# Turning the outputs of the first attention pair in the PSUM bank of another role

## The chip, the cores and the metric

One core of a Trainium2 chip runs the whole kernel as a single program. The metric is device time in microseconds (us), the median of several executions. One more execution is profiled. All durations below come from that one.

## The reference

The kernel computes one inference step of a small backbone: two layers (DEPTH = 2), model width 1024, on 128 context tokens and 512 latent tokens. A layer has four mixers side by side, whose outputs are concatenated and go through one projection `w_out`; then comes a gated feed-forward part.

```
h = rmsnorm(x, g_pre1) * (1 + scale1) + shift1
aq, ak, av, bq, bk, bv, cz, cx, cb, cc, cdt, du = split(h @ w_in)
ya = rmsnorm(diff_attention(aq, ak, av, lam), a_subln) * (1 - lam_init)   # 4 heads, two softmaxes each
yb = gqa_attention(bq, bk, bv)                                            # 4 query heads, 2 key heads
yc = ssd_mixer(cz, cx, cb, cc, cdt, ...)                                  # chunked scan, forward and backward
yd = s5_mixer(du, ...)
x = x + gate1 * rmsnorm(concat(ya, yb, yc, yd) @ w_out, g_post1)
h = rmsnorm(x, g_pre2) * (1 + scale2) + shift2
g, v = split(dwconv(h @ w_up))
x = x + gate2 * rmsnorm((silu(g) * v) @ w_down, g_post2)
```

## The kernel before

**The stages of a layer.** Projections from `w_in`, then the four mixers, then `w_out`, the norm, and the feed-forward part with `w_up` and `w_down`. The mixers are written one behind the other in `mixer` (S5, its GLU, `ssd` for the SSD scan, then `attention`), but they run interleaved: each piece of code carries a priority (`PR`: S5 0, GLU 10000, attention 20000, scan 30000, projections 40000; the smaller goes first), and a scheduler writes out one fixed list of instructions for each engine when the program is built. At run time each engine takes its list strictly in order.

**PSUM.** The eight banks are shared out by role (`pss`, L149): two of role p, two of role e, one of v, one of u, two of d. A request for a bank of a role gets the next buffer of that role in the order in which the requests stand in the code, and waits until the request that had this buffer last has been read out. So a request for d that `attention` makes stands behind every request for d that `ssd` made, whenever either runs. A matrix product of `ssd` goes to a bank of d throughout: the transposes of its inputs, eight state updates (L985 to L996), then for each of the five chunks of 128 tokens the scores, the decays and the outputs (L1003 to L1056), and last the sums and the spread of its norm.

**The attention.** It has six units (`units`, L1349): the first pair (0,0,0) and (0,0,1), two heads of the differential attention, below A0; then (1,0), two heads of the grouped attention, G0; then the second pair A1 and (1,1), G1. A unit is a list of fronts (scores, maxima, exponentials) and backs (transposes of the probabilities, products with the values). A back takes the probabilities in groups of four blocks of 128 by 128: four transposes into one bank (L1209, "weights turned"), a copy of the high part by ScalarE and of the low part by VectorE into SBUF (L155, L156), then eight products into the bank of role v. The bank of the weights comes from `self.tb`:

```
self.tb, self.work = itertools.cycle("u"), itertools.cycle([pool])
...
                if i == 3:
                    self.tb = itertools.cycle("ud")
```

So up to G0 all weights are turned in the single bank u; from A1 on (and in the last group of G0) u and d alternate. When the second head of a pair or of a G unit is done, its last back turns the outputs (`self.oo`, a tile `at_o` of which there is one buffer): four transposes into one bank, a fifth into the next (L1321), read by L1324 and L1325 into the rows of `h` that `w_out` multiplies. The next unit's first back (`prompt_back`) asks for `at_o` again, turns the weights of the prompt (`at_pp`, L1209), multiplies them in the same bank, and writes the result from the bank to `at_o` (`put`, L1223 and L1224). It can write only when the transposes of the outputs before have read `at_o`.

**What runs beside.** The first product with `w_out` (rows 6 and 4 of `h`: k = 6, 7 from S5, k = 4, 5 from the scan) and, in layer 0 alone, the modulation products (tile `wm`) fill TensorE in bank p.

Of the kernel before, what the change touches and what calls it, by code (L numbers as in the profile page):

```python
# [72 lines left out]
class K:  # L73
# [1069 lines left out]
    def attn_unit(self, l, pool, kq, kind, u, m0=0):  # L1143
# [61 lines left out]
        def turned(srcs, ps):  # L1205

            n = 128 * len(srcs)
            for j, s in enumerate(srcs):
                nc.tensor.transpose(ps[:, 128 * j:128 * j + 128], s, self.c("ident"))  # L1209
            w = next(self.work)  # L1210
            eh, el = (w.tile([P, 512], F32R, tag=t, name=t, bufs=2)[:, 0:n] for t in ("at_h", "at_l"))
            self.split(eh, el, ps[:, 0:n])
            return [(eh[:, 128 * j:128 * j + 128], el[:, 128 * j:128 * j + 128]) for j in range(len(srcs))]

        def values(o, e, kt, first, last):
            self.mm(o, e[0], vhl[:, kt, :], first, False)
            self.mm(o[:, 0:64], e[1], vhl[:, kt, 0:64], False, last)

        def put(O, ps):

            n = ps.shape[-1] // 128
            o = ps.rearrange("p (t x d) -> p t x d", t=n, x=2)
            A.copy(O, o[:, :, 0, :])  # L1223
            V.tensor_add(O, O, o[:, :, 1, :])  # L1224
# [4 lines left out]
        def small():  # L1229
            return pool.tile([P, 16], F32, tag="at_s", name="at_s", bufs=4)  # L1230
# [62 lines left out]
        def back(m, qt):  # L1293
            if qt == 0:
                st["out"], st["todo"] = self.pss("v"), []
            p, todo, out = st[m, qt], st["todo"], st["out"]
            todo += [(qt, kt, p[:, 128 * kt:128 * kt + 128]) for kt in range(5)]
            while len(todo) >= 4:
                group = todo[:4]
                del todo[:4]  # L1300
                for (t, kt, _), e in zip(group, turned([g[2] for g in group], self.pss(next(self.tb)))):
                    values(out[:, 128 * t:128 * t + 128], e, kt if kt < 4 else 5, kt == 0, kt == 4)
            if qt < 3:
                return
            o = O[m]
            put(o[:, 0:4, :], out)
            V.tensor_mul(o, o, rz[m].unsqueeze(2).to_broadcast([P, 5, 64]))
            if kind == 0:
                sq = pool.tile([P, 512], F32, tag="at_c", name="at_q")[:, 0:320].rearrange("p (t d) -> p t d", t=5)
                G.tensor_mul(sq, o, o)  # L1310
                ss = small()[:, 0:5]
                V.reduce_sum(ss, sq, axis=AX.X)
                r = self.rsqrt(pool, ss, 5, 64, "a")
                G.tensor_mul(o, o, r.unsqueeze(2).to_broadcast([P, 5, 64]))
            if m == 0:
                return
            for ts in ((0, 1, 2, 3), (4,)):
                ps = self.pss(next(self.tb))
                n = 128 * len(ts)
                for k, t in enumerate(ts):  # L1320
                    nc.tensor.transpose(ps[:, 128 * k:128 * k + 128], self.oo[:, t, :], self.c("ident"))  # L1321
                hi, lo = (t[:, CH[ts[0]]:CH[ts[0]] + n] for t in self.h[2 * u + kind])
                if kind == 0:
                    A.activation(hi, ps[:, 0:n], AF.Identity, scale=self.subg)  # L1324
                    V.scalar_tensor_tensor(lo, ps[:, 0:n], self.subg, hi.bitcast(F32), op0=ALU.mult, op1=ALU.subtract)  # L1325
                else:
                    self.split(hi, lo, ps[:, 0:n])
        return [(prompt_front, prompt_back)] + [(partial(front, m, qt), partial(back, m, qt)) for m in heads for qt in range(4)]

    @staticmethod  # L1330
# [480 lines left out]
```

## Time and profile before

| | us |
|---|---|
| median of 3 runs | 2189.75 |
| lowest and highest | 2186.13, 2194.58 |
| the profiled execution's own time | 2191.5 |
| its span, first to last instruction | 2189.7 |
| TensorE busy | 1956.1 (89%) |
| VectorE busy | 1245.6 (57%) |
| ScalarE busy | 802.4 (37%) |
| GpSimd busy | 676.4 (31%) |
| mean granted TensorE clock (1 is 2.4 GHz) | 0.898 |

The profile lists instructions by engine with start and duration, what ended an engine's idle time, and the chain of work that ended last, followed back from the end. A busy share is a mean over stages that have different limits. Here two stretches of the span are read, one in each layer, in which attention and scan run: 320 to 552 us and 1420 to 1650 us. In the lists PE is TensorE, DVE VectorE, ACT ScalarE and POOL GpSimd.

### The profile page before, as it was taken

The page shows a single profiled execution, that of the slowest core. Times are in us where ns is not written, and L with a number is a line of the kernel's source. Part 1 is how long each engine was busy: PE and PEld are TensorE (multiplying, and loading weights), DVE is VectorE, ACT ScalarE, POOL GpSimd, SP SyncE. Part 2 cuts the span into 40 slices and gives each one's busy share as a digit, 9 for nine tenths or more (in the row PEclk, how much of TensorE's full clock was granted, in tenths as well). Part 3 has the DMA queues.
Part 4 walks back from the last instruction along what each step waited for, and adds up shares of the span by engine and source line. Part 5 has one row for each costly group of instructions (what it writes and reads, how often), then busy time and mean ns, then how long its engine had stood idle before and what let it go on. Part 6 is the DMA issues. An engine that isn't in the chain of part 4 may idle for free.

```text
span 2189.7 us, 33260 instructions
## 1 busy us (share of the span) xinstructions
PE 1956.1 (89%) x12812; PEld 1786.6 (82%) x12812; DVE 1245.6 (57%) x2879; ACT 802.4 (37%) x1614; POOL 676.4 (31%) x723
## 2 busy tenths in 40 slices
PE   5996789999699999999988797897985999999997
PEld 2895775876597888999988786876875999999996
DVE  6876785475768575233366475653847631323345
ACT  3423353443452223232343244442444533313241
POOL 3553424200433352122244232323104332212232
PEclk9997789888799999999988887886866999999998
DMA  7464325134305665222224521310112012222221
GB/s 295 136 207 160 114 74 177 40 101 131 107 20 185 197 223 190 85 77 73 91 79 149 184 98 61 117 45 10 51 40 95 20 56 80 73 82 70 75 87 49
DMA packets 93511, 230.29 MB, mean 105 GB/s; under 512 B 17960, under 2 KB 30888, under 8 KB 93352
## 3 DMA queue, kind: packets, MB, share of 16 engines
q1 hardware_dynamic: 82856, 213.46, 29.8%
q10 hardware_dynamic: 10496, 14.71, 1.9%
q8 instruction: 101, 1.65, 0.3%
q14 instruction: 58, 0.48, 0.1%
HBM read 192.21 MB, written 35.92 MB: 104 GB/s over the span
## 4 chain that ended last, share of the span: by engine, by line
PE 67%; DVE 15%; DMA 9%; ACT 3%; issue 2%; POOL 2%; SPq 1%; ACTq 0%; POOLq 0%; DVEq 0%
PE psb L81 34%; PE psp L81 12%; PE psd L81 7%; PE pse L81 6%; PE psv L81 5%; DMA s_tb<-s5td 2%; DMA wm<-in_w_mod 1%; DVE nt L391 1%; PE psu L1209 1%; DMA wr<-in_w_down 1%; DVE x L394 1%; DMA ck<-in_cache_ak 1%; DVE wl L98 1%; DMA q<-d_bq 1%; DVE at_s L1279 1%
## 5 line engine op out<-in xcount | busy, mean ns | idle before, releaser
L81 PE MATMUL psb<-hh,wh 128*128 128x256 f32 (+1 forms) x1152 | 359.1, 312 | 2.3 <-DVE cv L451 2.3
L81 PE MATMUL psb<-hl,wh 128*128 128x256 f32 (+1 forms) x1152 | 358.3, 311 | 0.0
L81 PE MATMUL psb<-hh,wl 128*128 128x256 f32 (+1 forms) x1152 | 357.3, 310 | 0.0
L98 POOL TENSOR_TENSOR wl<-wr,wh 128x1024 fp32r<-128x1024 f32 (+3 forms) x87 | 192.3, 2211 | 502.7 <-ACT wh L95 451.6
L95 ACT CAST wh<-wr 128x1024 fp32r<-128x1024 f32 (+3 forms) x174 | 168.6, 970 | 417.9 <-PE psb L81 283.4
L81 PEld LDWEIGHTS psb<-hh,wh 128*128 128x128 f32 x1152 | 217.9, 189 | 13.3 <-issue 8.2
L81 PE MATMUL psp<-hh,wh 128*128 128x386 f32 (+1 forms) x640 | 215.3, 337 | 10.7 <-ACT hh L374 7.8
L81 PEld LDWEIGHTS psb<-hl,wh 128*128 128x128 f32 x1152 | 218.7, 190 | 3.4 <-issue 3.4
L81 PEld LDWEIGHTS psb<-hh,wl 128*128 128x128 f32 x1152 | 218.1, 189 | 3.4 <-issue 3.4
L81 PE MATMUL psp<-hl,wh 128*128 128x386 f32 (+1 forms) x640 | 209.8, 328 | 0.1
L81 PE MATMUL psp<-hh,wl 128*128 128x386 f32 (+1 forms) x640 | 207.0, 324 | 0.3 <-POOL wl L98 0.3
L98 DVE TENSOR_TENSOR wl<-wr,wh 128x1024 fp32r<-128x1024 f32 (+3 forms) x87 | 100.1, 1151 | 144.0 <-ACT wh L95 143.6
L81 PE MATMUL psb<-uh,wh 128*128 128x256 f32 (+1 forms) x544 | 169.9, 312 | 0.0
L81 PE MATMUL psb<-ul,wh 128*128 128x256 f32 (+1 forms) x544 | 169.4, 311 | 0.0
L81 PE MATMUL psb<-uh,wl 128*128 128x256 f32 (+1 forms) x544 | 169.1, 311 | 0.0
L81 PE MATMUL pse<-k,q 96*128 96x128 f32 (+5 forms) x288 | 107.1, 436 | 44.6 <-ACT at_p L1195 15.1
L81 PEld LDWEIGHTS psp<-hh,wh 128*128 128x128 f32 x640 | 129.0, 202 | 17.4 <-ACT hh L374 8.8
L81 PEld LDWEIGHTS psp<-hl,wh 128*128 128x128 f32 x640 | 129.3, 202 | 2.6 <-issue 1.1
L81 PEld LDWEIGHTS psp<-hh,wl 128*128 128x128 f32 x640 | 128.6, 201 | 1.4 <-issue 0.5
L1419 POOL TENSOR_TENSOR cv<-cv,cv 128x642 f32<-128x642 f32 x44 | 71.6, 1629 | 170.5 <-DVE cv L451 141.2
L81 PEld LDWEIGHTS pse<-k,q 96*128 96x128 f32 (+2 forms) x288 | 60.5, 229 | 77.7 <-issue 32.5
L450 DVE SCALAR_TENSOR_TENSOR cv<-psb,vec,cv 128x641 f32<-128x641 f32 x72 | 63.5, 881 | 103.2 <-ACT cv L449 103.2
(525 smaller groups left out, 4741.7 us busy)
## 6 DMA issues: line engine op xcount, KB each, us to landing
wm<-in_w_mod SPq DMA_DIRECT2D x96, 512.0 KB
wr<-in_w_up SPq DMA_DIRECT2D x88, 512.0 KB
wr<-in_w_in SPq DMA_DIRECT2D x30, 512.0 KB
wr<-in_w_down SPq DMA_DIRECT2D x32, 384.0 KB
wr<-in_w_down SPq DMA_DIRECT2D x32, 320.0 KB
wr<-in_w_out SPq DMA_DIRECT2D x16, 512.0 KB
s_tb<-s5td SPq DMA_DIRECT2D x8, 992.0 KB
s_to<-s5td SPq DMA_DIRECT2D x8, 768.0 KB
```

What stands on the lines that cost most here:

```text
L81: self.nc.tensor.matmul(out, w, x, start=start, stop=stop)
L95: nc.scalar.copy(hv, rv)
L98: e.tensor_sub(lv, rv, hv.bitcast(F32))
L391: nc.vector.scalar_tensor_tensor(t, y[c][:, t0:t1], gg[:, c, g:g + 1], r(t0, t1), op0=ALU.mult, op1=ALU.mult)
L394: (nc.gpsimd if c % 2 else nc.vector).tensor_add(xs, xs, t)
L450: nc.vector.scalar_tensor_tensor(out[:, 1:TW], x[:, 0:TW - 1], w[:, 0:1], out[:, 1:TW], op0=ALU.mult, op1=ALU.add)
L1209: nc.tensor.transpose(ps[:, 128 * j:128 * j + 128], s, self.c("ident"))
L1279: V.reduce_max(s[:, k:k + 1], ps, axis=AX.X)
L1419: G.tensor_mul(cv[0], cv[0], cv[1])
```

## The change

In the last back of a pair or G unit, the bank for the outputs of A0 (kind 0, u 0) is now asked of role d, and no longer of `self.tb`, which gives u there. Nothing else is written differently.

```
-                ps = self.pss(next(self.tb))
+                ps = self.pss("d" if kind == 0 and u == 0 else next(self.tb))
```

It concerns two banks and five transposes in each layer. The scheduler's lists move more than these. Three places on TensorE follow (psu, psd, psp are tiles in banks u, d and p; identr is the identity; at_o the outputs of A0; at_pp the weights of the prompt of G0; sd_, cf and nsq tiles belong to the scan, rq_y to its norm; wm to the modulation).

TensorE, layer 0, before: the outputs of A0 and the first weights of G0.

```order
L1321 MATMUL psu<-identr,at_o 128x128 x4
L81 MATMUL psd<-cst,sd_md 128x128 x4
L81 MATMUL pse<-k,q 128x128 x8
L81 MATMUL psp<-wm,sc 32x512 x2
L81 MATMUL psd<-sd_ex,sd_xd 64x128
L81 MATMUL psd<-cst,sd_small 64x128 x8
L1321 MATMUL psu<-identr,at_o 128x128
L81 MATMUL psp<-wm,sc 32x512 x2
L81 MATMUL psd<-sd_ex,sd_xd 64x128 x7
L81 MATMUL psd<-cf_2523,sd_h_3171 128x128
L81 MATMUL psd<-cf_2523,sd_h 128x128
L81 MATMUL psp<-wm,sc 32x512 x2
```

The outputs stand within the first chunk of the scan, and the first weights of G0 right behind.

TensorE, layer 0, with the change: the same outputs (hh_88 is row 4 of `h`, from the scan).

```order
L81 MATMUL psd<-cst,sd_md 128x128 x8
L81 MATMUL psd<-sd_ex,sd_xd 64x128 x8
L81 MATMUL psd<-cst,nsq 128x1 x10
L81 MATMUL psd<-identr,rq_y 128x128 x5
L1321 MATMUL psd<-identr,at_o 128x128 x4
L81 MATMUL psp<-hh_88,wh 128x256
L81 MATMUL psp<-hh_88,wh 128x386
L1321 MATMUL psd<-identr,at_o 128x128
L81 MATMUL psp<-hl_89,wh 128x256
L81 MATMUL psp<-hh_88,wl 128x256
L81 MATMUL psp<-hl_89,wh 128x386
L81 MATMUL psp<-hh_88,wl 128x386
```

The outputs now stand behind the last row of the scan's norm; in the list they moved from place 1219 to place 1369. The first weights of the prompt of G0 stand early, at 1204; its second ones, which stood at 1238, are at 1383, and all 40 blocks of probabilities of G0 follow them, with 96 rows of `w_out` (k = 4, 5) in between.

TensorE, layer 1, with the change: the end of the scan and the outputs of A0, which stood at place 6258 and 6405 before, the first weights of G0 at 6406.

```order
L81 MATMUL psd<-cf_13089,cf_12934 128x128 x2
L81 MATMUL psd<-cst,sd_md 128x128 x8
L81 MATMUL psd<-sd_ex,sd_xd 64x128 x8
L81 MATMUL psd<-cst,nsq 128x1 x10
L81 MATMUL psd<-identr,rq_y 128x128 x5
L1321 MATMUL psd<-identr,at_o 128x128 x4
```

The same turn of the order: outputs at 6549, the second weights of the prompt at 6563, then G0.

## Rows read from the trace of the kernel before

**Rows 1.** The page: the chain that ended last, shares by engine.

```profile
PE 67%; DVE 15%; DMA 9%; ACT 3%; issue 2%; POOL 2%; SPq 1%; ACTq 0%; POOLq 0%; DVEq 0%
```

**Rows 2.** Busy us by stretch: PE, PEld, DVE, ACT, POOL; granted clock, DMA share, GB/s.

```profile
409.40:433.80 24.40, 20.15 (x138) 17.58 (x138) 6.78 (x19) 9.29 (x22) 6.65 (x8) 0.86 0.07 22
433.80:446.00 12.20, 11.56 (x47) 10.94 (x47) 11.24 (x32) 5.73 (x17) 1.01 (x1) 0.50 0.01 2
446.00:513.60 67.60, 61.63 (x321) 38.91 (x319) 39.96 (x118) 28.33 (x92) 6.73 (x7) 0.88 0.43 134
513.60:551.60 38.00, 37.97 (x253) 35.05 (x253) 25.15 (x60) 16.34 (x39) 2.39 (x1) 0.89 0.35 110
1542.10:1609.70 67.60, 59.09 (x354) 52.68 (x352) 51.90 (x137) 31.70 (x95) 11.44 (x9) 0.88 0.15 49
```

**Rows 3.** Busy us by stretch of the weights turned alone (L1209): PE, PEld.

```profile
409.40:433.80 24.40, 0.64 (x4) 0.61 (x5) 0.86 0.07 22
...
1474.60:1530.70 56.10, 0.00 (x0) 0.20 (x1) 0.71 0.04 10
```

**Rows 4.** Timeline of PE, layer 0, attention: start, us, instruction, count.

```profile
344.03 0.66 PE L1321 MATMUL psu<-identr,at_o 128*128 128x128 f32 x4
...
349.58 0.33 PE L1321 MATMUL psu<-identr,at_o 128*128 128x128 f32 x1
...
409.38 0.66 PE L1209 MATMUL psu<-identr,at_p 128*128 128x128 f32 x4
...
433.80 1.06 PE L1209 MATMUL psd<-identr,at_p 128*128 128x128 f32 x4
...
446.04 1.06 PE L1321 MATMUL psu<-identr,at_o 128*128 128x128 f32 x4
...
513.64 1.11 PE L1321 MATMUL psu<-identr,at_o 128*128 128x128 f32 x4
...
551.60 0.63 PE L1321 MATMUL psu<-identr,at_o 128*128 128x128 f32 x4
```

**Rows 5.** Timeline of POOL and PE, layer 0, scan and first row of `w_out`.

```profile
328.99 1.18 POOL L971 TENSOR_TENSOR sd_xd<-sd_xt,sd_small 128x256 f32<-128x256 f32 x2 [0.99 <-DVE sd_small L946]
...
340.31 0.69 PE L81 MATMUL psd<-cf,cf 64*128 64x128 f32 x4
...
356.17 0.49 PE L81 MATMUL psd<-cf,cf 64*128 64x128 f32 x2
...
438.41 0.88 PE L81 MATMUL psp<-hh,wh 128*128 128x256 f32 x2
```

**Rows 6.** Timeline of PE, layer 1, attention.

```profile
1413.26 0.27 PE L1321 MATMUL psu<-identr,at_o 128*128 128x128 f32 x1
...
1427.38 1.12 PE L1209 MATMUL psu<-identr,at_p 128*128 128x128 f32 x4 [0.45 <-DVE at_o L1224]
...
1542.13 0.97 PE L1321 MATMUL psu<-identr,at_o 128*128 128x128 f32 x4
...
1648.48 1.09 PE L1321 MATMUL psu<-identr,at_o 128*128 128x128 f32 x4 [1.53 <-DVE at_o L1307]
```

**Rows 7.** Timeline of POOL and PE, layer 1, scan, and the first weights behind it.

```profile
1436.92 1.19 POOL L971 TENSOR_TENSOR sd_xd<-sd_xt,sd_small 128x256 f32<-128x256 f32 x2 [2.53 <-DVE sd_small L946]
...
1456.73 0.49 PE L81 MATMUL psd<-cf,cf 64*128 64x128 f32 x4
...
1476.73 0.48 PE L81 MATMUL psd<-cf,cf 64*128 64x128 f32 x2 [0.51 <-DVE sd_ea L1050]
...
1489.17 0.48 PE L81 MATMUL psd<-cf,cf 64*128 64x128 f32 x2 [0.51 <-DVE sd_ea L1050]
...
1530.71 1.06 PE L1209 MATMUL psd<-identr,at_p 128*128 128x128 f32 x4
```

**Rows 8.** Timeline of PE, layer 0: two rows of `w_out` that follow each other.

```profile
447.95 0.34 PE L81 MATMUL psp<-hh,wl 128*128 128x386 f32 x1
448.13 0.34 PE L81 MATMUL psp<-hh,wh 128*128 128x386 f32 x1
```

## The prediction

> **What bounds the kernel now.** I read the page first: TensorE carries 67% of the chain that ended last [rows 1]. That is a mean over the span, so I went on to the two stretches that the change touches, with the busy shares by stretch, and then to the timeline there. In layer 0 attention and scan run interleaved from about 340 us, where the scan's first chunk begins (340.31) [rows 5]. G0 (the grouped unit behind the first pair) turns its last single-bank group of weights at 409.38; the next group stands in bank d at 433.80 [rows 4]. In between VectorE works 6.78 of 24.40 us and ScalarE 9.29 [rows 2]; only four transposes of weights are in that stretch, those of 409.38, and in layer 1 there are none at all from 1474.6 to 1530.7 [rows 3]. The attention stands still there, because its next group asks for a bank of role d, and every request of the scan for d is ahead of it. As soon as the scan has ended, the attention goes on. So the end of this stage is set by the scan's end first, then by what is left of the attention: G0's outputs at 446.04, those of A1 at 513.64, those of G1 at 551.60 [rows 4]. In layer 1 the same chain reads 1530.71 [rows 7], 1542.13 and 1648.48 [rows 6]. From G0's outputs to those of G1 it is 105.6 us in layer 0 and 106.4 in layer 1. After that the last products with `w_out` and the norm wait for G1's outputs, so a shift of these passes on to the end.
>
> **What the change does.** It adds no instruction and takes none away: the same five transposes, copy and VectorE operation in each layer, in another bank. What it moves is a wait. The outputs of A0 need a bank of role d, and the requests of the scan for d come first in the code. So these transposes, which stood in the middle of the scan's first chunk, wait for the scan's last rows, as the list of TensorE shows. Behind them waits the single buffer `at_o`: the first back of G0 has multiplied its prompt weights early, but cannot write the result, and holds bank u meanwhile. All 40 blocks of probabilities of G0 are turned in that bank, or in d, so nearly all of G0 now runs after the scan, where before nine groups of ten ran beside it. The old wait of the attention before A1 goes away, because the scan is over by then; the new one, before G0, is longer. No DMA is added; on SP's queue the loads of `w_out` weights move with their rows, and I cost that at nothing, because the rows of k = 4, 5 wait for the scan's result in any case; if a load came late, it would show as idle time of TensorE behind the scan.
>
> **The scan's end.** Without G0 beside it the scan is faster. How fast it runs alone is seen in layer 1, after the attention stopped: one chunk takes 1489.17 - 1476.73 = 12.4 us, and the four last chunks with the norm take 1530.71 - 1476.73 = 54.0 us [rows 7].
> - Layer 0: the first chunk takes 356.17 - 340.31 = 15.9 us [rows 5], with the tail of A0 and the modulation beside it. That stays. The other four and the norm at the pace of layer 1: 356.2 + 54.0 = 410.2, against 433.80.
> - Layer 1: its state updates take from 1436.92 to 1456.73, 19.8 us, with G0 beside them [rows 7]; the same work takes 340.31 - 328.99 = 11.3 us in layer 0, with less of the attention beside it [rows 5]. So 1436.9 + 11.3 + 12.4 + 54.0 = 1514.6, against 1530.71.
> - Bounds: no gain at all (433.8 and 1530.7), since rows of `w_out` and of the modulation still stand between those of the scan; downwards some 3 us in each, if the first chunk in layer 0 takes 12.4 too.
>
> **G0 alone.** No row shows G0 with the scan over. The nearest is G1, a unit of the same kind with nothing but `w_out` beside it: from A1's outputs to its own 551.60 - 513.64 = 38.0 us [rows 4], TensorE busy all of it at a clock of 0.89 [rows 2]. Three things differ. Behind the scan the clock is low: the stretch of 12.2 us that follows it now is granted 0.50, that is 1.2 GHz, after a stretch in which the engine was partly idle [rows 2]; what takes 12.2 us there takes 6.9 at 0.89, so 5.3 more. TensorE's list then has rows of `w_out` that need the scan's own result; the first of them starts 438.41 - 433.80 = 4.6 us after the scan's end [rows 4, 5], and the second prompt weights stand behind it: 4.6 more. And the groups have one bank in place of two; I take 3 us. Sum 51. The other end is the length G0 has now: 409.38 - 349.58 = 59.8 us from A0's last output to the ninth group, and 446.04 - 433.80 = 12.2 for the rest [rows 4], 72 in all, with the scan beside it. The lower end is 38. I take 51, because G1 is the nearest row: the scan is over.
>
> **What follows.** From G0's outputs on everything stands as before: 105.6 and 106.4 us. The two stretches up to A1's outputs took 67.6 us both, although TensorE, VectorE and DMA had different work in them [rows 2], so I take them as a chain that does not mind what fills TensorE. The 96 rows of `w_out` that now run beside G0 leave this stretch; at 0.18 us a row at most (447.95 to 448.13 [rows 8]) that is 17 us of TensorE, which is the bound for a gain there. I take 0.
>
> **The sum.** Layer 0: 410.2 + 51 - 446.0 = 15.2 later. Layer 1: 1514.6 + 51 - 1542.1 = 23.5 later. Together 38.7 us. Against the profiled execution's own time of 2191.5 that gives 2230; the median of the runs shown is 1.75 below that execution, so 2189.75 + 38.7 = 2228. I predict **2228 us**. A difference of 0.5%, 11 us, is about what a measurement of this kernel can tell from no change.
>
> **Rivals.**
> - *G0 alone is as quick as G1.* Then it takes 38.0: layer 0 410.2 + 38.0 - 446.0 = 2.2, layer 1 1514.6 + 38.0 - 1542.1 = 10.5; 2202 us. For it: prompt scores and the first front of G0 are computed while it waits. Against it: the low clock behind the scan.
> - *G0 stays as slow as now.* 72 us: 42 more than the forecast, 2270 us. For it: in layer 0 modulation rows, whose weights come by DMA, fall between its groups. Against it: VectorE and ScalarE lose the scan's work.
> - *The new bank frees the attention: faster.* If the outputs got a buffer of d between two of the scan's requests, bank u would be free for G0's weights at once. In layer 0 the 5.6 us between the two output turns (344.03 and 349.58 [rows 4]) would go; in layer 1 G0 would no longer wait from 1413.26, the fifth output, to 1427.38, its first group [rows 6], and the scan would be alone sooner and end up to 16 us earlier (1514.6). 5.6 + 16 gives 2168 us. The Trainium skill (Perfetto Trace Analysis, section Matmuls) speaks for this: independent groups of matmuls should rotate through different banks, so that reading out one overlaps the next, and this change does that for outputs and weights; by that rule the sum would be 2168, by the rows it is 2228. The point that decides is whether the request waits behind the scan's. Here it does: the attention's next request for d waited until 433.80, though only four transposes ran in the 24.4 us before [rows 3, 4], and the lists put the outputs behind the norm. A bank that is another one is not a free one.
> - *Less filling in A1's stretch.* The 96 rows pay back all of their 17 us in each layer: 2228 - 34 = 2194, no change. Against it the two equal 67.6.
>
> **How the numbers follow.** Forecast, with G0 between 44 and 60 us: 0.60. G0 as quick as G1: 0.14. The filling pays back: 0.06. G0 as slow as now: 0.14. Freed attention: 0.06. The range leaves out the freed attention, the upper two thirds of the slow case and the lower part of the payback, under 0.2 in all: 2198 to 2258. Faster by over 0.5% is the freed attention alone, 0.06. Within 0.5% are the payback and over half of the quick case, whose 12.7 us lie at the limit: 0.14. Slower: 0.80.
>
> **What would show it.** In the timeline of TensorE after the change: the transposes at L1321 in bank d begin right after the scan's norm, near 410 in layer 0, and in layer 1 near 1515 plus the shift of layer 0; no group of weights (four transposes, `at_p`) of G0 stands between A0's outputs being ready and that moment; G0's outputs come some 51 us later; and A1's stretch is still near 67.6. That shift is 15 us. The prediction is wrong if transposes at L1321 in bank d start while products of the scan still follow, if the scan ends where it ended, or if G0 takes under 45 us.

## The result and the profile after

The changed kernel is slower by more than twice what was forecast: a median of 2298.72 us (2295.05 to 2302.01, 4 runs) against 2192.16 us (2186.13 to 2196.34, 4 runs) for the kernel before on the same chip, a ratio of 1.0488 with a 95% interval of 1.0455 to 1.0521. That is 107 us more; the forecast was 38, its range ended at 2258. The profiled executions differ by 2294.6 - 2189.7 = 104.9 us of span.

The page after has nearly the same work; TensorE's busy time grew by 40.5 us, at a lower mean clock (0.876, before 0.898).

```profile
span 2294.6 us, 33282 instructions
...
PE 1996.6 (87%) x12812; PEld 1814.8 (79%) x12812; DVE 1242.6 (54%) x2879; ACT 804.5 (35%) x1614; POOL 676.4 (29%) x723
...
PE 25%; DVE 2%; DMA 1%; POOL 1%; ACT 1%; issue 0%; POOLq 0%; DVEq 0%; ACTq 0%
```

The last line answers to [rows 1], but can't be set beside it: the chain that ended last is followed back here only as far as 1593.44 us, to the norm of layer 1's scan, so its shares add up to 30%. What follows is read from the timeline instead. It shows first that the wait is where it was forecast. TensorE, layer 0, timeline (start, us, engine, line, operation, out<-in, shapes, count, and in brackets the idle time before):

```profile
418.69 2.72 PE L81 MATMUL psd<-cst,nsq 128*128 128x1 f32 x12 [0.25 <-ACT nsq L309]
421.26 2.97 PE L81 MATMUL psd<-identr,rq_y 128*128 128x128 f32 x10
424.02 1.06 PE L1321 MATMUL psd<-identr,at_o 128*128 128x128 f32 x4
...
428.55 0.27 PE L1209 MATMUL psu<-identr,at_pp 128*128 128x128 f32 x1
...
434.45 0.60 PE L1209 MATMUL psu<-identr,at_p 128*128 128x128 f32 x4
```

The outputs of A0 are turned 424.02 us into the span, right behind the scan's norm, where before it was 344.03 [rows 4]. The second prompt weights of G0 and its first group follow. The busy time of the weights turned alone says the same of the stretch ahead: none from 380 to 424, then all of G0's.

```profile
380.00:424.00 44.00, 0.00 (x0) 0.83 0.12 37
424.00:491.50 67.50, 7.65 (x41) 0.86 0.35 104
```

Then the stretches that answer to [rows 2]. In each row: bounds, length, busy us (count) of PE, PEld, DVE, ACT and POOL, then granted clock, DMA share and GB/s. The first two are G0 in layer 0, then A1 and G1; the last three are G0, A1 and G1 in layer 1.

```profile
424.00:434.40 10.40, 9.62 (x50) 7.45 (x49) 8.94 (x24) 4.60 (x14) 0.00 (x0) 0.88 0.01 2
434.40:491.50 57.10, 45.99 (x255) 29.25 (x254) 25.69 (x69) 19.72 (x60) 1.00 (x1) 0.85 0.41 122
491.50:579.30 87.80, 60.48 (x295) 48.76 (x293) 43.91 (x127) 31.42 (x92) 11.50 (x9) 0.69 0.20 63
579.30:618.30 39.00, 35.47 (x153) 31.23 (x153) 15.54 (x37) 13.01 (x35) 0.00 (x0) 0.54 0.19 62
1594.90:1649.20 54.30, 48.42 (x260) 40.40 (x258) 38.28 (x104) 28.08 (x82) 3.39 (x2) 0.78 0.12 36
1649.20:1712.30 63.10, 53.49 (x266) 45.04 (x265) 40.13 (x112) 27.72 (x84) 8.61 (x8) 0.72 0.10 35
1712.30:1751.20 38.90, 35.37 (x153) 31.06 (x152) 15.53 (x37) 13.00 (x35) 0.00 (x0) 0.54 0.19 62
```

In layer 0 A1's stretch takes 87.8 us and holds only 60.5 of TensorE's work; before it took 67.6 and held 61.6. So 20 us of standing still have come in where the forecast put nothing. The timeline names them; the first of these rows lies in G0's stretch, the second in A1's:

```profile
461.67 1.92 PE L81 MATMUL psp<-wm,sc 128*32 128x512 f32 x4 [6.43 <-DMA wm<-in_w_mod]
...
517.68 1.92 PE L81 MATMUL psp<-wm,sc 128*32 128x512 f32 x4 [18.81 <-DMA wm<-in_w_mod]
```

TensorE, which takes its list in order, stands 6.4 and 18.8 us before rows of the modulation whose weights have not landed. SP's queue shows what is ahead of the last of these weights:

```profile
450.76 40.89 SPq L226 DMA_DIRECT2D wm<-in_w_mod  x13
491.74 0.53 SPq L1182 DMA_DIRECT2D q<-d_bq  x1
492.96 0.52 SPq L1174 DMA_DIRECT2D k<-d_bk  x1
493.52 5.19 SPq L1175 DMA_DIRECT2D k<-d_bk  x1
498.75 0.51 SPq L1182 DMA_DIRECT2D q<-d_bq  x1
499.36 6.89 SPq L226 DMA_DIRECT2D wm<-in_w_mod  x1
```

Thirteen of the 14 modulation loads of this part are issued ahead of the q and k of G1, the last one right behind them. In the kernel before all 14 stand behind the same four loads, but the first is issued 17 us after the fourth; TensorE's longest wait for modulation weights is 1.6 us there:

```profile
446.27 0.54 SPq L1182 DMA_DIRECT2D q<-d_bq  x1
...
451.82 0.65 SPq L1182 DMA_DIRECT2D q<-d_bq  x1
469.53 34.59 SPq L226 DMA_DIRECT2D wm<-in_w_mod  x14
```

And the loads of q and k are slow: two windows of the changed kernel from the time in which they move (same columns as above) show idle engines and a DMA share of 0.13, which is two of 16 DMA engines, at 50 GB/s.

```profile
501.50:506.00 4.50, 0.00 (x0) 0.00 (x0) 0.00 (x0) 0.00 (x0) 0.00 (x0) 0.50 0.13 50
509.60:515.00 5.40, 0.00 (x0) 0.00 (x0) 0.00 (x0) 0.00 (x0) 0.00 (x0) 0.50 0.13 51
```

Layer 1 has the same thing in another place. On SP's queue three loads of q now stand ahead of a store of the new keys, which stood ahead of them before (1408.26 and 1411.12 us), and ScalarE, which needs the stored tile's buffer, waits 9.7 us; the scan's inputs are made behind it. First SP, then ScalarE:

```profile
1483.38 2.31 SPq L1166 DMA_DIRECT2D q<-d_aq  x3
1485.79 0.87 SPq L1130 DMA_DIRECT2D out_new_ak<-raw  x1
...
1496.97 0.74 ACT L456 ACTIVATE raw<-cz 128x642 f32<-128x642 f32 x1 [9.74 <-DMA out_new_ak<-raw]
```

**The theory** after this reading has two parts. First the forecast one: outputs in bank d wait for the scan, the single buffer `at_o` holds G0 back until then. Second a new one: in the new order slow loads of q and k stand ahead of transfers that an in-order engine needs. **The rivals**: any bank other than u costs; the long stretches are due to the filling work that was moved there; the scan is slow by its own chain.

### The profile page after: what moved, and what is told of

Read it like the earlier page. It is cut to its first block, busy times and chain, and to the rows that moved or that the text cites. A ratio compares the mean times of both kernels' runs of the same rounds, so it can differ in the third digit from the quotient of the medians.

```text
span 2294.6 us, 33282 instructions
## 1 busy us (share of the span) xinstructions
PE 1996.6 (87%) x12812; PEld 1814.8 (79%) x12812; DVE 1242.6 (54%) x2879; ACT 804.5 (35%) x1614; POOL 676.4 (29%) x723
## 5 line engine op out<-in xcount | busy, mean ns | idle before, releaser
L81 PE MATMUL psp<-hh,wh 128*128 128x386 f32 (+1 forms) x640 | 216.4, 340 | 16.5 <-ACT hh L374 7.8
L81 PE MATMUL pse<-k,q 96*128 96x128 f32 (+5 forms) x288 | 116.3, 468 | 47.8 <-ACT at_p L1195 23.6
```

Of the source, the lines that this page charges most:

```text
L81: self.nc.tensor.matmul(out, w, x, start=start, stop=stop)
```

## The experiments

Each kernel was timed against the kernel before on its own chip. "Over before" is the ratio less one, times 2192 us, so that chips can be compared.

| kernel | median us | before there | ratio, 95% interval | us over before |
|---|---|---|---|---|
| the change | 2298.72 | 2192.16 | 1.0488 (1.0455 to 1.0521) | 107 |
| change in layer 0 alone | 2262.89 | 2192.47 | 1.0317 (1.0293 to 1.0341) | 69 |
| change in layer 1 alone | 2224.13 | 2192.47 | 1.0147 (1.0119 to 1.0176) | 32 |
| outputs in bank v | 2224.55 | 2192.47 | 1.0128 (1.008 to 1.0177) | 28 |
| outputs in bank e | 2218.89 | 2192.47 | 1.012 (1.0096 to 1.0143) | 26 |
| change, modulation half left out | 2250.86 | 2193.85 | 1.0273 (1.024 to 1.0305) | 60 |
| before, modulation half left out | 2189.44 | 2193.85 | 0.9975 (0.9955 to 0.9996) | -5 |
| change, loads cut up | 2211.3 | 2193.85 | 1.0081 (1.0056 to 1.0106) | 18 |
| before, loads cut up | 2152.31 | 2193.85 | 0.9816 (0.9789 to 0.9844) | -40 |
| change, second buffer | 2230.28 | 2186.17 | 1.0199 (1.0175 to 1.0223) | 44 |
| change, loads cut up, second buffer | 2156.22 | 2186.17 | 0.9857 (0.9822 to 0.9893) | -31 |
| bank v, loads cut up | 2155.0 | 2186.17 | 0.9858 (0.9835 to 0.988) | -31 |
| change, rows k = 4, 5 first | 2267.07 | 2186.17 | 1.037 (1.0345 to 1.0394) | 81 |
| change, G loads alone cut up | 2267.72 | 2198.69 | 1.0329 (1.0291 to 1.0367) | 72 |
| change, A loads alone cut up | 2246.89 | 2198.69 | 1.0228 (1.019 to 1.0265) | 50 |
| before, loads cut up, rows k = 4, 5 first | 2173.39 | 2198.69 | 0.9884 (0.9846 to 0.9921) | -25 |

### One layer at a time

```
-                ps = self.pss("d" if kind == 0 and u == 0 else next(self.tb))
+                ps = self.pss("d" if kind == 0 and u == 0 and l == 0 else next(self.tb))
```

and the same with `l == 1`.

> The change in layer 0 alone; layer 1 asks its outputs' bank as before. Theory (outputs behind the scan, G0 after it, and late modulation weights in A1's stretch): the changed kernel's trace moves layer 0 by +66.7 us between the scan and G1's outputs, so 2192 + 67 = 2259 us (2252 to 2270), with A1's stretch near 88 us and layer 1 as before: outputs of A0 in bank u, A1's stretch 67.6, scan's end to G1's outputs 118. Rival (the loss comes of something that both layers share, such as scratch traffic or the clock, and does not split by layer): well away from 2259, and layer 1 also changed by over 5 us.

> The change in layer 1 alone. Theory: the changed kernel's trace moves layer 1 by +33 to +36 us, so 2192 + 35 = 2227 us (2220 to 2236), with no wait of TensorE for modulation weights over 2 us in layer 0, and G0 alone in layer 1 near 54 us. The two layers alone add up to the whole: (this minus before) + (layer 0 alone minus before) within 8 us of 106. Rival (layer 0's delay makes layer 1 worse): under 2215.

Both came as the theory had it, 69 and 32 us; together 101 of the 107. With layer 0 alone A1's stretch there is 85.6 us and that of layer 1 67.3; with layer 1 alone G0's stretch there is 54.3, as in the full change. The layers don't act on one another by more than the measurement can tell.

### Another bank, not behind the scan

```
-                ps = self.pss("d" if kind == 0 and u == 0 else next(self.tb))
+                ps = self.pss("v" if kind == 0 and u == 0 else next(self.tb))
```

and the same with `"e"`.

> The outputs of A0 are turned in the bank of role v (one buffer, the attention's own), so apart from the bank of the weights as in the change, but not behind the scan's requests. Theory (it is the place behind the scan that costs, not the other bank): outputs of A0 stay within the scan's first chunk in layer 0, within 10 us of 344; 2180 to 2200 us, within 0.5% of before. Rival A (any bank away from the weights' bank costs, since the outputs and the prompt weights then collide elsewhere): 2220 or more. Rival B (the freed weights' bank gives what the prediction's third rival gave): near 2168.

> The outputs of A0 in a bank of role e (two buffers, those of the scores and of the scan's shared work in the attention). Theory: no request of the scan stands ahead of it, so 2175 to 2210 us; the list shows the outputs at nearly their old place. The fronts of G0 rotate through the same two banks, so a few us of G0's scores may come later. Rival A (any other bank costs): 2220 or more. Rival B (freed weights' bank helps): near 2168.

A miss for the theory in both: 28 and 26 us slower than before, although the outputs of A0 stand within the scan's first chunk (340.91 us with bank v, 336.95 with bank e). That looks like the first rival. But the timeline of the kernel with bank v has, in layer 0, TensorE idle for 8 us before the first filling row of `w_out`; ScalarE, which rounds its weights, waits 10.9 us for their load, and on SP's queue loads of q and k stand ahead of it, where in the kernel before the first two loads of `w_out` were issued ahead of those:

```profile
371.98 0.71 SPq L1167 DMA_DIRECT2D k<-d_ak  x1
372.73 0.69 SPq L1166 DMA_DIRECT2D q<-d_aq  x1
373.47 0.68 SPq L1167 DMA_DIRECT2D k<-d_ak  x1
...
375.13 2.15 SPq L88 DMA_DIRECT2D wr<-in_w_out  x2
```
```profile
387.67 1.04 ACT L95 CAST wh<-wr 128x1024 fp32r<-128x1024 f32 x1 [10.89 <-DMA wr<-in_w_out]
```
```profile
388.77 0.58 PE L81 MATMUL psp<-hh,wh 128*128 128x256 f32 x1 [8.08 <-ACT wh L95]
```

The trace of bank e has the same wait before the same row, with 5.61 us. So this could also be the second part of the theory. The runs with the loads cut up decide it for bank v. The profiled execution with bank v took 2205.72 us, beside a median of 2224.55, so its trace shows only part of the 28 us.

### The modulation left out

```
-                            if l == 0:
+                            if l == 0 and i == 0:
+                                nc.vector.memset(self.mod[0][:, 32:48, :], 0.0)
                                 with self.prio(p):
```

> The changed kernel without the second half of layer 0's modulation (the rows of tile wm that run beside attention and scan; scale2 and gate2 of layer 0 are set to zero in their place). Theory (in layer 0 TensorE stands 6.4 us in G0's stretch and 18.8 us in A1's for modulation weights that come late, because the loads of G1's q and k now stand ahead of them on SP's queue): the difference to the kernel before with the same rows left out falls from 106 to about 80 us (72 to 90), A1's stretch in layer 0 from 87.8 to about 68. Rival (A1's stretch is long because the fill that is left runs in it, of whatever kind, or the clock is low): the difference stays above 95 and A1's stretch above 80.

> The kernel before without the same half of layer 0's modulation, as the base for the run above. 14 loads and some 100 rows at up to 0.25 us fewer: 5 to 40 us faster than before, 2150 to 2187 us. Theory and rival do not differ here; they differ in the distance to the run above.

A1's stretch in layer 0 fell to 60.2 us, and the distance of the two kernels from 107 to 61 us, more than expected. The rows are worth 5 us in the kernel before (its interval ends just short of no difference, at 0.9996) and 47 in the changed one: the same filling is free in one order and dear in the other. Part of what was gained beyond the two waits is in G1's stretch, 28.9 us in place of 39.0; more on that below. This run takes the rows away together with their loads, so it can't tell a late load from filling work by itself; the next two runs keep the rows.

### The loads of q and k cut up

```
-                nc.sync.dma_start(q[i][0:96].bitcast(F32), self.qd[f"aq{u}"][:, f:f + 32])
+                for j in range(3):
+                    nc.sync.dma_start(q[i][32 * j:32 * j + 32].bitcast(F32), self.qd[f"aq{u}"][j, f:f + 32])
...
-            nc.sync.dma_start(k1[:, 0:TW].bitcast(F32), self.qd["bk"][0:2, r])
+            for j in range(2):
+                nc.sync.dma_start(k1[64 * j:64 * j + 64, 0:TW].bitcast(F32), self.qd["bk"][j, r])
```

and alike for the other two. The same bytes move, in two or three transfers in place of one.

> The changed kernel with every load of q and k of the attention cut into one transfer for each block of 32 or 64 rows (the blocks of the outermost dimension, 2 or 3, now one transfer each). Theory (the loads of 321 KB go at some 51 GB/s, a DMA share of 0.11, because a transfer with an outermost dimension of 2 or 3 is spread over few of the 16 engines; cut up, each block spreads over more, and the loads behind them on the queue come on time): waits of TensorE for wm and of ScalarE for out_new_ak go, 25 us in layer 0 and some 8 in layer 1: 2258 to 2280 us. Rival (the loads are slow for another reason, their rows or where they come from): 2290 to 2305 us, and the DMA share of these loads stays near 0.11.

> The kernel before with the same loads cut up in the same way. Theory: in the kernel before no wait of TensorE for modulation weights is over 1.2 us, so there is little to gain: 2180 to 2195 us, and the distance to the run above falls to about 80 us. Rival (slow loads cost in both alike): both fall by the same amount, and their distance stays near 106.

The cause of the slow loads is as the theory had it. In the changed kernel with cut loads, the stretch in which G1's q and k move has 0.98 of all engines at 282 GB/s (the modulation load issued at 483.48 us moves in it too):

```profile
480.20:487.50 7.30, 5.99 (x36) 3.48 (x35) 6.52 (x23) 4.71 (x18) 0.00 (x0) 1.00 0.98 282
```

The sizes were off, upwards: the changed kernel gains 89 us, not 25 to 33, and the kernel before 40, where next to nothing was expected, because I had looked in it for waits on the modulation alone. The waits of TensorE in the kernel before, summed by line (us in total, times, longest), show some of it: rows of scores that wait for k and q themselves, which with cut loads are no longer among its largest waits.

```profile
PE pse L81 <- DMA k<-d_ak: 13.9, 2, 8.4
...
PE pse L81 <- DMA q<-d_bq: 8.4, 2, 5.9
```

The distance of change and before is 2.65% now, 58 us. In the changed kernel with cut loads G0's, A1's and G1's stretches in layer 0 are 58.8, 66.5 and 28.7 us (columns as above):

```profile
420.10:478.90 58.80, 51.77 (x304) 36.02 (x303) 34.73 (x93) 24.41 (x74) 1.00 (x1) 0.95 0.40 120
478.90:545.40 66.50, 55.39 (x296) 43.69 (x294) 43.83 (x127) 31.52 (x92) 11.48 (x9) 0.82 0.27 83
545.40:574.10 28.70, 25.04 (x152) 21.16 (x152) 15.25 (x37) 12.86 (x35) 0.00 (x0) 0.80 0.25 83
```

So without slow loads A1's stretch does stand where the forecast left it (67.6), with the modulation rows still in it: the filling work alone did not make it long.

### Which of the loads

Only the loads of the grouped units cut up (`bk`, `bq`), or only those of the differential units (`aq`, `ak`).

> The changed kernel with the loads of q and k of the grouped units (bq, bk) alone cut up. Theory (their place ahead of the last modulation loads is what makes TensorE wait 6.4 and 18.8 us in layer 0): A1's stretch in layer 0 falls from 87.8 to under 72 us, layer 1 stays; 2262 to 2280 us. Rival (it is the loads of the differential units that matter): 2290 or more, A1's stretch still above 80.

> The changed kernel with the loads of the differential units (aq, ak) alone cut up. Theory: the waits for modulation weights in layer 0 stay (A1's stretch above 80), while in layer 1 the wait of ScalarE for out_new_ak (9.7 us) goes and the scan there ends 10 to 35 us earlier against the layer's start; 2230 to 2265 us. The gains of the two runs add up to that of all loads, 87 us, within 15. Rival: little gain, 2285 or more.

With G loads cut, 35 us of 107 go: the wait of 18.8 us is no longer there and A1's stretch is 66.2 us. But the wait of 6.4 us in G0's stretch stays:

```profile
463.20 1.92 PE L81 MATMUL psp<-wm,sc 128*32 128x512 f32 x4 [6.36 <-DMA wm<-in_w_mod]
```

With A loads cut, 57 us go, and it is the other way round: G0's stretch is 59.3 us, A1's stretch is 87.8, and its wait stays:

```profile
511.92 1.92 PE L81 MATMUL psp<-wm,sc 128*32 128x512 f32 x4 [18.80 <-DMA wm<-in_w_mod]
```

In layer 1 the wait for the store of the keys has gone, and from the first prompt weights of the layer to the outputs of A0 it is 1543.42 - 1308.16 = 235.3 us in place of 1594.92 - 1324.33 = 270.6. The gains add up, 92 us beside 89 for all loads. So the first reading is mended in one place: the wait of 6.4 us belongs to the loads of A1, that of 18.8 to those of G1.

### A second buffer for the outputs

```
-                self.oo = pool.tile([P, 5, 128], F32, tag="at_o", name="at_o")
+                self.oo = (self.ao if kind == 1 and u == 0 else pool).tile([P, 5, 128], F32, tag="at_o", name="at_o")
...
+            self.ao = left.enter_context(self.pool(f"ao{l}", "right"))
             with self.pool(f"sd{l}", "right") as sd, self.prio(base + PR["ssd"]):
```

> The changed kernel with a second buffer for the outputs: G0 writes its own tile, in a pool of its own on the right side, A0 and the others share the old one. The outputs of A0 still stand behind the scan in bank d. Theory (the link between the late outputs and G0 is the single buffer at_o): G0 runs beside the scan again, its outputs in layer 0 come within 15 us of 446, A1's stretch is back near 68; 2180 to 2225 us (other orders of the same rows moved the time by up to 32 us, so no closer). Rival (G0 waits for the scan for another reason, the bank u that holds its prompt weights or the row order in d): 2270 to 2300, G0's outputs in layer 0 still behind 485.

> The same second buffer in the changed kernel with the loads of q and k cut up (2211 us). Theory: without the link through at_o, what is left of the change with quick loads, 59 us against the kernel before with the loads cut up (2152 us), goes: 2145 to 2172 us. Rival: 2195 to 2215.

With cut loads this is clear: the outputs of A0 still stand behind the scan, G0's follow 14.5 us later in place of 58.8, and the time is 2156 us, 49 of the 58 us gone. The remaining 9 us can't be told from nothing (the intervals overlap). First the outputs of A0, then the first of G0's:

```profile
428.68 0.63 PE L1325 MATMUL psd<-identr,at_o 128*128 128x128 f32 x2
...
443.23 0.38 PE L1325 MATMUL psu<-identr,at_o 128*128 128x128 f32 x2
```

With the loads as they were the outcome is 2230 us, just above what was expected, and G0's outputs come at 469.75, not by 461. G0 does run beside the scan again (17.4 us from A0's outputs at 452.31 to its own), but in the new order TensorE waits in the middle of the scan for modulation weights, and A1's stretch is 72.8 us:

```profile
377.39 1.92 PE L81 MATMUL psp<-wm,sc 128*32 128x512 f32 x4 [8.46 <-DMA wm<-in_w_mod]
```

So the single buffer is shown to be the link that holds G0 back, and not bank u or the order in d, which are the same in these kernels.

### Bank v with cut loads

> Outputs of A0 in the bank of role v, with the loads of q and k cut up. Theory (the 32 us that bank v cost against before is TensorE's wait of 8.1 us for the first w_out weights, whose loads stand behind three loads of q and k, and later ones of the same kind; not the bank): 2140 to 2165 us, within 0.6% of the kernel before with loads cut up (2152). Rival (bank v or any bank other than u costs by itself): 2175 to 2190, the old distance of 32 us kept.

The time is 2155.0 us, beside 2152.31 for the kernel before with cut loads (the intervals overlap). Against before, each on its own chip, that is -31 beside -40 us: of the 28 us of bank v at most some 9 are left, which can't be told from nothing, and the rest were the loads. The first rival has fallen for v. For bank e, which cost 26 us, this wasn't tried; the wait in its trace is of the same kind, but what it costs there is not shown.

### What fills the scan

```
-            for k in (6, 4):
+            for k in (4, 6):
...
-                if ws[0][0] == 6:
+                if ws[0][0] == 4:
```

> The changed kernel with the two halves of the first w_out product in the other order: rows k = 4, 5 first, which need the scan's result, so that no row of w_out can fill the scan. Theory on the scan's end (forecast 410 in layer 0, measured 424 because some 24 us of w_out rows k = 6, 7 and modulation rows now stand between the scan's own): scan's norm ends 8 to 14 us earlier in layer 0, 412 to 416, and G0 or A1 takes the same rows later; 2275 to 2310 us in all. Rival (the scan is as slow by its own chain): norm's end within 3 us of 424.

> A candidate: the kernel before with loads cut up and the two halves of the first w_out product in the other order (rows that need the scan first). In the changed kernel this order brought the scan's end 9 us forward in layer 0 and 20 us in layer 1 against the layer's start, and 32 us in all. Theory (what fills the scan delays it, whichever kernel): 2130 to 2150 us. Rival (in the kernel before these rows fill gaps that G0 leaves, and are missing later): 2155 to 2180 us.

In the changed kernel the outputs of A0 come at 415.3 us in layer 0, 8.7 earlier, and in layer 1 250.8 us after the layer's first prompt weights, 19.8 earlier. So in layer 0 most of what the scan's end missed the forecast by is filling rows of `w_out` between its own. In layer 1 this isn't shown: the new order also moved the loads, and ScalarE's wait for the store of the keys is gone in this trace. The time fell by 26 us, more than expected; in layer 0 the wait of 6.4 us in G0's stretch has gone with it too, while one of 16.5 us in A1's stretch stays. And it is a property of that kernel: in the quickest one, the kernel before with cut loads, the same order costs 15 us (0.9884 and 0.9816; the intervals, 0.9846 to 0.9921 and 0.9789 to 0.9844, lie just apart), as its rival had it.

**The quickest version** is thus the kernel before with the loads of q and k cut up: 2152.31 us, 0.9816 of before (0.9789 to 0.9844). It beats both kernels, and has nothing of the change in it. Bank v and the second buffer with cut loads (2155.0 and 2156.22 us) can't be told from it.

## Why the prediction was wrong in size

The sign and the mechanism were right: the request waits behind the scan's last, TensorE turns no weights of G0 from 380 to 424 us, and the single buffer `at_o` is the link. Three terms of the sum were too small. Layer 1 is counted from its own start here, which came 69.5 us later.

| step of the prediction | layer 0: forecast, measured | layer 1: forecast, measured | missed by, us |
|---|---|---|---|
| scan's end | 410.2, 424.0 | 1514.6, 1525.4 | 13.8 + 10.8 |
| G0 alone | 51, 67.5 | 51, 54.3 | 16.5 + 3.3 |
| what follows: A1 | 67.6, 87.8 | 67.6, 63.1 | 20.2 - 4.5 |
| what follows: G1 | 38.0, 39.0 | 38.8, 38.9 | 1.0 + 0.1 |

That makes 61.2, and between the layers and after them another 5.0; with the forecast 38.7 it is 104.9, the difference of the two spans.

- **"What follows" failed, in layer 0.** I had taken the 67.6 us of A1 in both layers as a chain that does not mind what fills TensorE, and the move of DMA loads on SP's queue as free, because I looked for those of `w_out` k = 4, 5 alone. The modulation rows had moved too: nearly all of them now run in G0's stretch, and the last of their loads stands right behind the q and k of G1, not 17 us after them. That is the 18.8 us, and with these loads cut up the stretch is 66.2 us. The sign that the forecast gave for a late load, idle time of TensorE behind the scan, came true. The forecast asked of the requests for a bank who stands ahead, and did not ask it of this queue: the four loads of q and k stood in the order on SP, and their slowness in the trace of the kernel before, with a DMA share of 0.13 at 50 GB/s from 462 to 466 us.
- **G0 alone** was near in layer 1, 54.3 for 51, though partly by luck. Of the terms added to G1's 38.0, the wait for the first rows of `w_out` came as forecast, 428.55 - 424.02 = 4.5 us for 4.6. The low clock right behind the scan did not: the first 10.4 us in layer 0 were granted 0.88, not 0.50. The 3 us for one bank no run shows. In layer 0 6.4 of the missing 16.5 us are the wait behind the q and k of A1; with A loads cut up it is 59.3 us, with all 58.8, and with the modulation rows left out 54.2, as in layer 1. The rival of a slow G0 had named modulation rows between G0's groups; in layer 0 it was nearer, at 67.5 of its 72 us, for a reason that it had half.
- **The scan's end** was sized from layer 1's chunks with little filling. In layer 0 the filling does not go away with the attention: it moves in, and 8.7 of the 13.8 us go with the order of the `w_out` rows. In layer 1 part of the 10.8 is the wait of 9.7 us for the store of the keys: with A loads cut up the outputs come 35 us earlier in the layer. How the 10.8 divide there stays open.
- **The sum's rest** held in kind, not in size. With quick loads in both kernels the change costs 58 us by the medians, half as much again as the forecast 38.7 (45.5 by the two profiled spans); a second buffer takes 49 of these back. The other 49 of the 107 us go when the loads are quick, so they belong to slow loads in the new order, with what the clock of G1's stretch adds in layer 0 (below).
- **The rivals.** G0 as quick as G1, the filling that pays back and the freed attention did not come. The rule of the Trainium skill (Perfetto Trace Analysis, section Matmuls) to rotate groups through different banks gave 2168 us as a mechanism; no run here shows a gain by another bank for the outputs, neither v nor d nor, with uncut loads, e.

## What to carry to other kernels

A bank of another role is free only if its queue of requests is: look up who asks before. When a change moves rows in a list that an engine takes in order, go through the DMA queue as well, and ask of each slow transfer what now stands behind it and which engine will wait for that; a kernel can hide a slow load for as long as nothing urgent is behind it. A slow load that is found so is better mended than moved around.

## What was not expected of the hardware

A load into 128 rows whose source has an outermost dimension of two moved at 50 GB/s with a DMA share of 0.13, two of 16 engines; as two transfers, one for each block, the stretch reached 282 GB/s and a share of 0.98, with a modulation load beside them. Loads with an outermost dimension of three moved at 75 and 76 GB/s with a share of 0.20 and 0.19, three of 16: the first window here has the q of a differential unit in it, the second the k, both in layer 1 of the changed kernel.

```profile
1493.00:1497.00 4.00, 0.00 (x0) 0.00 (x0) 0.00 (x0) 0.03 (x1) 0.00 (x0) 0.73 0.20 75
1509.00:1513.00 4.00, 0.00 (x0) 0.00 (x0) 3.48 (x20) 0.00 (x0) 0.00 (x0) 0.50 0.19 76
```

The Trainium skill states this (DMA: Bandwidth & Descriptors, section Rules for kernel authors): an outermost dimension smaller than 16 keeps the whole transfer on at most that many engines. The traces agree with it, by the shares of 0.13 and 0.19; I had not held the loads of the trace of before against it.

G1's stretch, with 152 or 153 rows of TensorE, took 38.8 to 39.0 us wherever its granted clock was 0.54, 40.4 where it was 0.50, and 28.7 to 28.9 where it was 0.80. Of the rows below the first is layer 1 of the kernel before, the second layer 1 of the kernel with bank v.

```profile
1609.70:1648.50 38.80, 35.27 (x153) 30.87 (x152) 15.53 (x37) 13.00 (x35) 0.00 (x0) 0.54 0.19 62
```
```profile
1632.60:1661.40 28.80, 25.16 (x152) 21.25 (x151) 15.34 (x37) 12.87 (x35) 0.00 (x0) 0.80 0.25 83
```

At 0.54 TensorE runs near 1.2 GHz, the lower of its two levels, through most of the stretch. The stretch before was busy to 56.8 of 65.1 us at 0.92 in the second case, in the kernel before to 59.1 of 67.6 at 0.88 [rows 2]. These runs don't tell what decides between the two. In layer 0 of the changed kernel the higher level came back in all three profiled executions with the 18.8 us of waiting gone (modulation left out, all loads cut up, G loads cut up), and that is 10 us of their gain. The level may also differ between executions of one kernel: those profiled with bank v and with G loads cut up took 19 and 13 us less than the median of their kernel; that the level is the reason is not shown. My 38.0 for G1 [rows 4], with 100 rows more at a clock of 0.89, was therefore no price of its own chain alone.
